# Moving the last pair sums of w_down out of the gates-and-branches stage of a fused attention and feed-forward block

## The chip, the cores and the metric

The kernel runs on one core of one Trainium2 chip. The metric is the device time of one execution in microseconds (us), the median over several runs. Each core has a TensorE (PE) for matrix products, VectorE (DVE), ScalarE (ACT), GpSimd (POOL) and SyncE (SP); all work from their own queues of instructions, in order, and wait for one another by semaphores. In this kernel SP does nothing but issue transfers between the chip's large memory (HBM) and the on-chip memory, one queue of them in program order.

## The reference

One layer of a hybrid block on 256 tokens of width 2048, all in float32:

```
h = rms_norm(x, g_mix); proj = h @ w_in            # queries, keys, values, gates
o_fox = forgetting attention, 6 heads               # softmax with a decaying bias
o_sb  = stick-breaking attention, 6 heads
o_mem = attention over 256 memory tokens, 4 heads
g = sigmoid(gates + b_gate)                          # three gates of width 2048
merged = g0 * (o_fox @ w_br_fox) + g1 * (o_sb @ w_br_sb) + g2 * (o_mem @ w_br_mem)
x = x + merged @ w_out
h2 = rms_norm(x, g_ffn)
u = causal_depthwise_conv(h2 @ w_up)                 # 3 taps, 11264 channels
x = x + (silu(u_gate) * u_val) @ w_down              # w_down is 5632 x 2048
```

## The kernel before

Every float32 product is made of three faster products: a weight tile `raw` is rounded on ACT to `hi` (L143, L379), DVE takes the rest `lo = raw - hi` (L144, L380), and PE multiplies hi by hi, hi by lo and lo by hi into one accumulator (`three`, L385 to L387; the up stage, L1365 and L1366, leaves a part out). So a weight tile goes through four queues: SP loads it into one of four `raw` buffers, ACT and DVE make `hi` and `lo` in four buffers each, PE uses them. SP may load tile n+4 only when DVE is done with tile n, and ACT may make `hi` n+4 only when PE is done with n.

The stages follow one another on PE: the memory's keys and values (`kv`), the projections `mq`, `f0` to `f4` (forgetting), `s0` to `s4` (stick-breaking; `s4`, the last, is half as wide), the first products of the branches `b`, six gate blocks `g` with the other branch products between and after them, `w_out` (`o`), the up stage (`u`, 22 groups of 4 x 128 channels, 8 pairs of weight rows each), and `w_down` (`d`).

**Pair sums.** In `o` and `d` (and in the gates) some pairs of weight row-tiles ("pairs") are multiplied with seven block products in place of eight, by the scheme of Strassen and Winograd. This wants sums of the blocks of the weights. For `o` and `d` they are made long before: a pair of 128 x 1024 weight tiles (1 MB) is loaded into a staging tile, DVE makes the four sums with three additions (`sums_in`, L254 to L256), and the tile is written back to HBM (`kept_d...`), from where the stages `o` and `d` load it (L473, L476, L478). 37 pairs are made so; the last two of `d` are summed by transfers alone (`sums_in_hbm`). The queue `halves` fixes their order: first 10 pairs of `o`, then `d` 0, 1, 2 and so on.

A **tick** is one step of the weight loop: each `product` calls `tick()` once per loaded piece, and each generator in `background` then makes one step. Three of them eat from `halves`, after one pair (`first_sums`) in the projection `mq`:

- `pair_sums_ahead(in_turn, PF, 3, 7, most=14)` in the projections `f` and `s`: a new pair every 6 or 5 ticks in turn (`PF`), loaded into one of the two halves of `staged`, its sums 3 ticks after the load, its store 7 ticks after it.
- `half_sums(..., 6, 2, 4, ...)` beside the gates and branches: half a pair at a time (two loads of 256 KB, three shorter additions, one store of 512 KB), four times, in the tile with the tag `pre`, which the stage `o` uses later as one of its `raw` buffers.
- `pair_sums_ahead(ends_tile, (15,) + (8,) * 20, 1, 5, delay=DU)` in the up stage: the first pair at tick 7, the second 15 ticks later, then one every 8 ticks; sums 1 tick and store 5 ticks after the load. There is one staging tile (`ends`, named `pre_d...`), so a load waits until the store before it has landed.

A scheduler sets each engine's order from the program's order and its own estimates; what goes through `in_order` or `pin` keeps its place among its like.

In the first steps of the up stage the kernel also computes the rows' norm of `x` (L632 to L637), writes it to HBM (`rstd_row`, L1233, 1 KB, a POOL transfer) and reads it back spread over all partitions (`rbc`, L1234). The first convolutions (L1310) need `rbc`.

Of the kernel before, what the change touches and what calls it, by code (L numbers as in the profile page):

```python
# [10 lines left out]
F32 = mybir.dt.float32  # L11
# [5 lines left out]
P = 128  # L17
# [18 lines left out]
SBUFS = 4  # L36
BLOCKS = 14
GS = 3
PF = (6, 5)
DU = 7  # L40


@with_exitstack
def hybrid_block(
# [57 lines left out]
    background = []  # L102
# [18 lines left out]
    def until(*names):  # L121
        while not issued.issuperset(names):
            yield
# [128 lines left out]
    def sums_in(w):  # L252
        both = w[:, 1:2].to_broadcast([P, 2, w.shape[2]])
        in_order(nc.vector.tensor_tensor(w[:, 0:2], w[:, 0:4:3], both, ALU.add))  # L254
        in_order(nc.vector.tensor_tensor(w[:, T2], w[:, T1], w[:, T2], ALU.add))
        in_order(nc.vector.tensor_tensor(w[:, T4], w[:, T2], w[:, T4], ALU.add))  # L256

    def kept_for(name, nb, pr):
        if (name, nb, pr) not in sums_of:
            at = f"kept_{name}{nb}_{pr}"  # L260
            sums_of[name, nb, pr] = dram.tile([P, 4, 512], F32, tag=at, name=at)
        return sums_of[name, nb, pr]

    def half_sums(staging, period, add, store, starts):

        for start in starts:
            yield from until(*start)
            name, wv, nb, pr, h = halves.popleft()
            kept = kept_for(name, nb, pr)
            w = staging(f"pre_{name}{nb}_{pr}_{h}").rearrange("p (i c) -> p i c", i=4)  # L270
            n0 = nb * PIECE + h * 256
            for n in range(2):
                in_order(
                    nc.sync.dma_start(
                        w.rearrange("p (k n) c -> p k n c", k=2)[:, :, n],
                        wv[:, 2 * pr : 2 * pr + 2, n0 + n * 512 : n0 + n * 512 + 256],
                    )
                )
            for _ in range(add):
                yield  # L280
            sums_in(w)
            for _ in range(store - add):
                yield
            in_order(nc.sync.dma_start(kept[:, :, h * 256 : (h + 1) * 256], w))
            for _ in range(period - store):
                yield

    def pair_sums_ahead(staging, period, add, store, most=99, delay=0):

        due = deque()  # L290
        clock = 0
        for _ in range(delay):
            yield

        def step():
            while due and due[0][0] <= clock:
                _, kept, w = due.popleft()
                in_order(nc.sync.dma_start(kept, w))

        periods = cycle(period if isinstance(period, tuple) else (period,))  # L300
        while len(halves) > 1 and halves[0][-1] == 0 and most:
            most -= 1
            name, wv, nb, pr, _ = halves.popleft()
            halves.popleft()
            kept = kept_for(name, nb, pr)
            w = staging(f"pre_{name}{nb}_{pr}")
            in_order(
                nc.sync.dma_start(
                    w.rearrange("p (k c) -> p k c", k=2), wv[:, 2 * pr : 2 * pr + 2, nb * PIECE : (nb + 1) * PIECE]
                )  # L310
            )
            w = w.rearrange("p (i c) -> p i c", i=4)
            due.append((clock + store, kept, w))
            for t in range(next(periods)):
                if t == add:
                    sums_in(w)
                step()
                clock += 1
                yield
        while due:  # L320
            step()
            clock += 1
            yield
# [342 lines left out]
    gp = mix.enter_context(tc.tile_pool(name="gp", bufs=3))  # L666

    def block(name, dt=F32):
        return bp.tile([P, 1024], dt, tag="blk", name=name)

    def heads_of(b):
        return b.rearrange("p (h s) -> p h s", h=4)
# [212 lines left out]
        turn[0] += 1  # L885
        return staged[:, turn[0] % 2]

    background.append(pair_sums_ahead(in_turn, PF, 3, 7, most=14))
    qm = [heads_of(block(f"qm_{i}", F32R)) for i in "hl"]
    y = norm_heads(ps, rstd, "mq")  # L890
    later(heads_T(y, qm[0], (gh[:, 2:3], gh[:, 2:3]), 2, "mq", qm[1]))
# [182 lines left out]
    def x_sums():  # L1074
        yield
        for p in range(GS):
            pair_sums(xT.pair(p), (junk(f"xa_{p}"), junk(f"xr_{p}")), [(xs[:, p], slice(0, 4))])
            for _ in range(3):
                yield

    background.append(x_sums())
    background.append(
        half_sums(lambda name: gp.tile([P, 1024], F32, tag="pre", bufs=1, name=name), 6, 2, 4, ((), (), ("second",), ()))
    )


    mT = [None] * (KT // 2)
# [164 lines left out]
    for nb, plan in enumerate(o_plans):  # L1252
# [18 lines left out]
    ends = []  # L1271
    ends_tile = lambda name, dt: ff.tile([P, 2, PIECE], dt, tag="ends", bufs=1, name=name)
    background.append(
        pair_sums_ahead(lambda name: ends_tile(name, F32).rearrange("p i c -> p (i c)"), (15,) + (8,) * 20, 1, 5, delay=DU)
    )
    a_done = []
    background.append(last_sums(148, 12))
# [72 lines left out]
    for f0 in range(0, FT, 4):  # L1350
# [5 lines left out]
        for s in range(2):  # L1356
            ps = [bank(f"u{f0 + i}_{s}") for i in range(4)]
            c0 = s * D_FF + f0 * P
            for k in range(0, KT, 2):
                hi, lo = piece(upv[:, k : k + 2, c0 : c0 + 512], 2, 512, f"u{f0}_{s}_{k}")  # L1360
                for j in range(2):
                    first, last = k + j == 0, k + j == KT - 1
                    for i in range(4):
                        c = slice(i * P, (i + 1) * P)
# [63 lines left out]
    for nb, plan in enumerate(d_plans):  # L1428
# [5 lines left out]
        for t in range(NT):  # L1434
            for n in range(2):
                c = nb * PIECE + n * 512
                o = xres[:, t, c : c + 512]
                nc.vector.tensor_tensor(o, o, X[t][n], ALU.add)
                if (nb, t, n) == (1, 1, 1):
                    nc.scalar.dma_start(ov[:, t, c : c + 256], o[:, :256])  # L1440
                    c, o = c + 256, o[:, 256:]
# [35 lines left out]
```

## Time and profile before

| what | value |
|---|---|
| runs | median 1453.27 us of 3 (1453.22 to 1453.76) |
| the profiled execution | 1453.81 us, of it 1452.1 us from the first to the last instruction (span) |
| granted TensorE clock | 1.000 |
| PE busy | 1447.0 us, 100% of the span |
| PE loading weights | 1225.8 us, 84% |
| DVE busy | 1247.5 us, 86% |
| ACT busy | 870.1 us, 60% |
| transfers | 393.41 MB, mean 271 GB/s |
| `pre_d` loads of half_sums | 8 of 256 KB, median 4.0 us from issue to landing |
| `pre_d` loads of the up stage | 18 of 1024 KB, median 7.4 us |
| `kept_d` stores of the up stage | 18 of 1024 KB, median 6.1 us |

The profile is of one execution. Its own time, 1453.81 us, is 1.7 us more than its span and 0.5 us above the median of the runs. In a row such as `L254 DVE TENSOR_TENSOR pre_d<-pre_d x22: 677/1218/1221, 313.0 to 1152.1`, the parts are the line, the engine, the operation, the tile written and the tile read, the count, the shortest, middle and longest duration in ns, and the starts of the first and the last in us. In a timeline row the first number is the start, the second the duration, both in us, and brackets hold the idle time of the engine before it with what ended it.

### The profile page before, as it was taken

What the parts mean: (1) busy time and instruction counts of PE and PEld (TensorE: products, weight loads), DVE (VectorE), ACT (ScalarE), POOL (GpSimd) and SP (SyncE); (2) the same over time, 40 slices, a digit from 0 to 9 for tenths busy, and PEclk for the clock granted to TensorE, in tenths of its full rate; (3) what the DMA queues carried; (4) which work ended last, traced back from release to release, by engine and by line L of the source; (5) the groups of instructions that cost most, each with busy time, mean ns of one, the idle gap of its engine ahead of it and who ended that gap; (6) DMA issues with size and microseconds to landing.
All of it is one profiled execution on the core that took longest, in us unless ns stands there. A gap on an engine that the chain in (4) does not pass through costs nothing.

```text
span 1452.1 us, 20709 instructions
## 1 busy us (share of the span) xinstructions
PE 1447.0 (100%) x7298; PEld 1225.8 (84%) x7298; DVE 1247.5 (86%) x1851; ACT 870.1 (60%) x1248; POOL 32.3 (2%) x70
## 2 busy tenths in 40 slices
PE   9999999999999999999999999999999999999998
PEld 7888888888888888888888888888888888888887
DVE  5888778777999999998897888888888877999988
ACT  6755445465555555546676656556556556676775
POOL 0000011010000000000000000000000011000000
PEclk9999999999999999999999999999999999999999
DMA  8797899775677676788877888888888899789996
GB/s 296 228 350 269 309 336 321 266 250 182 214 219 230 202 219 207 265 267 278 289 231 264 302 273 292 284 267 303 288 275 298 274 252 262 251 286 345 317 341 236
DMA packets 165783, 393.41 MB, mean 271 GB/s; under 512 B 12859, under 2 KB 28111, under 8 KB 161327
## 3 DMA queue, kind: packets, MB, share of 16 engines
q1 hardware_dynamic: 162190, 384.86, 79.3%
q0 software_dynamic: 2160, 5.12, 1.8%
q10 hardware_dynamic: 1328, 2.11, 0.4%
q8 instruction: 57, 0.93, 0.2%
q14 instruction: 48, 0.39, 0.1%
HBM read 353.24 MB, written 43.00 MB: 273 GB/s over the span
## 4 chain that ended last, share of the span: by engine, by line
PE 98%; DMA 1%; ACT 0%; DVE 0%; issue 0%; DVEq 0%; ACTq 0%
PE u L1365 22%; PE u L1366 11%; PE xg L387 5%; PE xg L386 5%; PE xg L385 5%; PE xd L387 3%; PE xd L386 3%; PE xd L385 3%; PE s L385 2%; PE s L387 2%; PE f L385 2%; PE f L386 2%; PE f L387 2%; PE s L386 2%; PE b L387 2%; PE b L386 2%
## 5 line engine op out<-in xcount | busy, mean ns | idle before, releaser
L1365 PE MATMUL u<-hT,hi_u 128*128 128x512 f32 x1232 | 428.4, 394 | 0.0
L1366 PE MATMUL u<-hT,lo_u 128*128 128x256 f32 x1232 | 341.3, 277 | 0.0
L1365 PEld LDWEIGHTS u<-hT,hi_u 128*128 128x128 f32 x1232 | 231.0, 188 | 53.6
L144 DVE TENSOR_TENSOR lo_u<-raw_u,hi_u 128x1024 fp32r<-128x1024 f32 x176 | 215.1, 1222 | 69.4 <-ACT hi_u L143 69.3
L143 ACT CAST hi_u<-raw_u 128x1024 fp32r<-128x1024 f32 x176 | 184.6, 1050 | 131.5 <-PE u L1365 105.1
L1366 PEld LDWEIGHTS u<-hT,lo_u 128*128 128x128 f32 x1232 | 231.3, 188 | 0.0
L379 ACT CAST hi_g<-raw_g 128x1024 fp32r<-128x1024 f32 (+1 forms) x96 | 92.5, 973 | 54.0 <-PE xg L386 23.7
L380 DVE TENSOR_TENSOR lo_d<-raw_d,hi_d 128x1024 fp32r<-128x1024 f32 x88 | 106.8, 1222 | 12.3 <-ACT hi_d L379 6.9
L379 ACT CAST hi_d<-raw_d 128x1024 fp32r<-128x1024 f32 x88 | 91.7, 1054 | 35.8 <-PE xd L386 12.2
L380 DVE TENSOR_TENSOR lo_g<-raw_g,hi_g 128x1024 fp32r<-128x1024 f32 (+1 forms) x96 | 106.4, 1119 | 4.1 <-ACT hi_g L379 3.6
L385 PE MATMUL xg<-hi_g,xT 128*128 128x512 f32 x210 | 82.0, 390 | 0.0
L387 PE MATMUL xg<-lo_g,xT 128*128 128x512 f32 x210 | 81.8, 389 | 0.0
L386 PE MATMUL xg<-hi_g,xT 128*128 128x512 f32 x210 | 81.7, 389 | 0.0
L379 ACT CAST hi_t_g<-t_g 128x1024 fp32r<-128x1024 f32 x36 | 37.9, 1053 | 48.7 <-PE xg L386 41.4
L143 ACT CAST hi_f<-raw_f 128x1024 fp32r<-128x1024 f32 (+1 forms) x40 | 38.6, 968 | 39.9 <-PE f L386 23.7
L1365 PE MATMUL u<-hT_rest,hi_u 128*128 128x512 f32 x176 | 62.0, 394 | 0.0
L144 DVE TENSOR_TENSOR lo_s<-raw_s,hi_s 128x1024 fp32r<-128x1024 f32 (+1 forms) x40 | 44.6, 1123 | 18.5 <-ACT hi_s L143 18.5
L1315 ACT ACTIVATE y<-u,taps 128x256 f32<-128x256 f32 x88 | 49.6, 596 | 17.5 <-DVE u L1310 17.4
L143 ACT CAST hi_s<-raw_s 128x1024 fp32r<-128x1024 f32 (+1 forms) x40 | 38.3, 960 | 32.5 <-PE s L386 19.5
L380 DVE TENSOR_TENSOR lo_t_g<-t_g,hi_t_g 128x1024 fp32r<-128x1024 f32 x36 | 43.6, 1221 | 14.7 <-ACT hi_t_g L379 14.6
L144 DVE TENSOR_TENSOR lo_f<-raw_f,hi_f 128x1024 fp32r<-128x1024 f32 (+1 forms) x40 | 44.4, 1117 | 13.8 <-ACT hi_f L143 13.6
L379 ACT CAST hi_t_d<-raw_t_d 128x1024 fp32r<-128x1024 f32 (+1 forms) x54 | 43.5, 835 | 19.1 <-PE xd L386 11.7
(556 smaller groups left out, 3496.3 us busy)
## 6 DMA issues: line engine op xcount, KB each, us to landing
raw_u<-in_w_up_dram SPq DMA_DIRECT2D x176, 512.0 KB, 5.0
raw_g<-in_w_in_dram SPq DMA_DIRECT2D x96, 512.0 KB, 4.4
raw_d<-in_w_down_dram SPq DMA_DIRECT2D x61, 512.0 KB, 5.6
pre_d<-in_w_down_dram SPq DMA_DIRECT2D x18, 1024.0 KB, 7.4
kept_d<-pre_d SPq DMA_DIRECT2D x18, 1024.0 KB, 6.1
raw_f<-in_w_in_dram SPq DMA_DIRECT2D x32, 512.0 KB, 5.8
raw_s<-in_w_in_dram SPq DMA_DIRECT2D x32, 512.0 KB, 6.1
raw_t_d<-kept_d SPq DMA_DIRECT2D x27, 512.0 KB, 6.7
```

Source lines behind the costliest of these rows:

```text
L143: pin(nc.scalar.copy(hi[:, :m], raw[:, :m]))
L144: pin(nc.vector.tensor_tensor(lo[:, :m], raw[:, :m], hi[:, :m].bitcast(F32), ALU.subtract))
L379: nc.scalar.copy(hi[:, :n], src)
L380: nc.vector.tensor_tensor(lo[:, :n], src, hi[:, :n].bitcast(F32), ALU.subtract)
L385: fix(nc.tensor.matmul(o, lhsT=ah, rhs=w[0], start=first, stop=False))
L386: fix(nc.tensor.matmul(o, lhsT=al, rhs=w[0], start=False, stop=False))
L387: fix(nc.tensor.matmul(o, lhsT=ah, rhs=w[1], start=False, stop=last))
L1315: nc.scalar.activation(y, u[:, 2:], AF.Identity, scale=tap(2), bias=tap(3))
L1365: nc.tensor.matmul(ps[i], lhsT=hi[:, j, c], rhs=hT(k + j), start=first, stop=False)
L1366: nc.tensor.matmul(ps[i][:, :S], lhsT=lo[:, j, c], rhs=hT(k + j)[:, :S], start=False, stop=last)
```

## The change

Three numbers and one line change. The two pairs that `half_sums` made beside the gates and branches are made elsewhere: the generator in the projections makes 15 pairs in place of 14, and the one in the up stage 19 in place of 18.

```
-PF = (6, 5)
-DU = 7
+PF = (6, 5) * 5 + (6,) + (5,) * 4
+DU = 6
...
-    background.append(pair_sums_ahead(in_turn, PF, 3, 7, most=14))
+    background.append(pair_sums_ahead(in_turn, PF, 3, 7, most=15))
...
-    background.append(
-        half_sums(lambda name: gp.tile([P, 1024], F32, tag="pre", bufs=1, name=name), 6, 2, 4, ((), (), ("second",), ()))
-    )
...
-        pair_sums_ahead(lambda name: ends_tile(name, F32).rearrange("p i c -> p (i c)"), (15,) + (8,) * 20, 1, 5, delay=DU)
+        pair_sums_ahead(lambda name: ends_tile(name, F32).rearrange("p i c -> p (i c)"), (7, 9) + (8,) * 20, 1, 5, delay=DU)
```

In ticks: the pairs of the projections start at the same ticks as before up to the thirteenth, the fourteenth (`d` 4) one tick earlier, and the new fifteenth (`d` 5) five ticks after it, in `s4`. In the up stage the pairs start at ticks 6, 13, 22, 30 and so on, before at 7, 22, 30 and so on; so `d` 6 and `d` 7 stand where `d` 7 alone stood, and from `d` 8 on nothing moves. Line numbers above 1082 are smaller by 3 in the changed kernel.

PE's instructions stand in the same order before and after. On the other engines two places differ most.

**The end of the stick-breaking projections.** SP's queue there, before (`raw_s` are tiles of `s4`, `raw_b` of the first branch products, `staged` a pair's load, `kept_d_4` its store, `pre_d_5_0` the first half-pair):

```order
L142 DMA raw_s_8_2994<-in_w_in_dram 128x2x256
L142 DMA raw_s_10_3012<-in_w_in_dram 128x2x256
L142 DMA raw_s_12_3030<-in_w_in_dram 128x2x256
L142 DMA raw_s_14_3048<-in_w_in_dram 128x2x256
L142 DMA raw_b_0_0_3073<-in_w_br_fox_dram 128x2x512
L298 DMA kept_d_4_2925<-staged 128x2048
L274 DMA pre_d_5_0_3092<-in_w_down_dram 128x2x256 x2
L142 DMA raw_b_0_2_3107<-in_w_br_fox_dram 128x2x512
```

And now:

```order
L142 DMA raw_s_8_2994<-in_w_in_dram 128x2x256
L308 DMA staged<-in_w_down_dram 128x2x1024
L142 DMA raw_s_10_3014<-in_w_in_dram 128x2x256
L142 DMA raw_s_12_3032<-in_w_in_dram 128x2x256
L298 DMA kept_d_4_2884<-staged 128x2048
L142 DMA raw_s_14_3051<-in_w_in_dram 128x2x256
L142 DMA raw_b_0_0_3079<-in_w_br_fox_dram 128x2x512
L142 DMA raw_b_0_2_3109<-in_w_br_fox_dram 128x2x512
L142 DMA raw_b_0_4_3168<-in_w_br_fox_dram 128x2x512
L142 DMA raw_b_0_0_3191<-in_w_br_fox_dram 128x2x512
L142 DMA raw_b_0_2_3209<-in_w_br_fox_dram 128x2x512
L298 DMA kept_d_5_3012<-staged 128x2048
```

The load of pair `d` 5 stands three tiles of `s4` ahead of the first branch tiles, and its store after five of them. DVE at the same place, before:

```order
L144 TENSOR_TENSOR lo_s_10_3014<-raw_s_10_3012,hi_s_10_3013 128x512
L144 TENSOR_TENSOR lo_s_12_3032<-raw_s_12_3030,hi_s_12_3031 128x512
L144 TENSOR_TENSOR lo_s_14_3050<-raw_s_14_3048,hi_s_14_3049 128x512
L144 TENSOR_TENSOR lo_b_0_0_3075<-raw_b_0_0_3073,hi_b_0_0_3074 128x1024
L403 TENSOR_TENSOR xs<-xr_3126,xs 128x4x128
```

And now:

```order
L144 TENSOR_TENSOR lo_s_10_3016<-raw_s_10_3014,hi_s_10_3015 128x512
L144 TENSOR_TENSOR lo_s_12_3034<-raw_s_12_3032,hi_s_12_3033 128x512
L144 TENSOR_TENSOR lo_s_14_3053<-raw_s_14_3051,hi_s_14_3052 128x512
L254 TENSOR_TENSOR staged<-staged 128x1024
L255 TENSOR_TENSOR staged<-staged 128x512
L144 TENSOR_TENSOR lo_b_0_0_3081<-raw_b_0_0_3079,hi_b_0_0_3080 128x1024
L256 TENSOR_TENSOR staged<-staged 128x512
L144 TENSOR_TENSOR lo_b_0_2_3111<-raw_b_0_2_3109,hi_b_0_2_3110 128x1024
```

Two of the three sums of `d` 5 stand ahead of the first branch tile's `lo`.

**The first steps of the up stage.** SP before (`raw_u_1_*` are the weights of the second half-group of the first four channel tiles; `raw_t_d` loads kept sums for `w_down` ahead of time):

```order
L142 DMA raw_u_1_6_7190<-in_w_up_dram 128x2x512
L478 DMA raw_t_d_0_12107<-kept_d_0_2285 128x512
L478 DMA raw_t_d_1_12198<-kept_d_1_2443 128x512
L142 DMA raw_u_1_8_7212<-in_w_up_dram 128x2x512
L142 DMA raw_u_1_10_7235<-in_w_up_dram 128x2x512
L298 DMA kept_d_7_7098<-pre_d_7_7099 128x2048
L142 DMA raw_u_1_12_7257<-in_w_up_dram 128x2x512
L142 DMA raw_u_1_14_7284<-in_w_up_dram 128x2x512
```

And now:

```order
L478 DMA raw_t_d_0_12090<-kept_d_0_2285 128x512
L478 DMA raw_t_d_1_12181<-kept_d_1_2443 128x512
L142 DMA raw_u_1_6_7166<-in_w_up_dram 128x2x512
L142 DMA raw_u_1_8_7189<-in_w_up_dram 128x2x512
L298 DMA kept_d_6_7052<-pre_d_6_7053 128x2048
L142 DMA raw_u_1_10_7211<-in_w_up_dram 128x2x512
L142 DMA raw_u_1_12_7236<-in_w_up_dram 128x2x512
L308 DMA pre_d_7_7234<-in_w_down_dram 128x2x1024
L142 DMA raw_u_1_14_7266<-in_w_up_dram 128x2x512
```

The load of `d` 7, which waits for the store of `d` 6 to land, now stands ahead of `raw_u_1_14`. (The first load, of `d` 7 before and of `d` 6 now, stands one tile earlier, ahead of `raw_u_0_14`.) DVE before:

```order
L144 TENSOR_TENSOR lo_u_0_14_7078<-raw_u_0_14_7076,hi_u_0_14_7077 128x1024
L635 TENSOR_TENSOR nwt_f<-nwy_f 128x2
L636 SCALAR_TENSOR_TENSOR nwt_f<-nwt_f,nwa_f 128x2
L637 SCALAR_TENSOR_TENSOR scales<-nwt_f,nwy_f 128x2
L144 TENSOR_TENSOR lo_u_1_0_7107<-raw_u_1_0_7105,hi_u_1_0_7106 128x1024
L254 TENSOR_TENSOR pre_d_7_7099<-pre_d_7_7099 128x1024
L255 TENSOR_TENSOR pre_d_7_7099<-pre_d_7_7099 128x512
L144 TENSOR_TENSOR lo_u_1_2_7142<-raw_u_1_2_7140,hi_u_1_2_7141 128x1024
L256 TENSOR_TENSOR pre_d_7_7099<-pre_d_7_7099 128x512
```

Now, first around the same tiles and then, further on, around `lo_u_1_14`:

```order
L144 TENSOR_TENSOR lo_u_0_14_7057<-raw_u_0_14_7055,hi_u_0_14_7056 128x1024
L254 TENSOR_TENSOR pre_d_6_7053<-pre_d_6_7053 128x1024
L635 TENSOR_TENSOR nwt_f<-nwy_f 128x2
L255 TENSOR_TENSOR pre_d_6_7053<-pre_d_6_7053 128x512
L636 SCALAR_TENSOR_TENSOR nwt_f<-nwt_f,nwa_f 128x2
L144 TENSOR_TENSOR lo_u_1_0_7086<-raw_u_1_0_7084,hi_u_1_0_7085 128x1024
L637 SCALAR_TENSOR_TENSOR scales<-nwt_f,nwy_f 128x2
```

```order
L144 TENSOR_TENSOR lo_u_1_12_7238<-raw_u_1_12_7236,hi_u_1_12_7237 128x1024
L254 TENSOR_TENSOR pre_d_7_7234<-pre_d_7_7234 128x1024
L255 TENSOR_TENSOR pre_d_7_7234<-pre_d_7_7234 128x512
L144 TENSOR_TENSOR lo_u_1_14_7268<-raw_u_1_14_7266,hi_u_1_14_7267 128x1024
L256 TENSOR_TENSOR pre_d_7_7234<-pre_d_7_7234 128x512
```

The norm of the rows (L637) now comes after two sums and one `lo`, and the sums of `d` 7 stand ahead of `lo_u_1_14`.

Between these places the twelve transfers and twelve additions of `half_sums` are gone. With the tile `pre` free earlier, one 512 KB load of stage `o` (`raw_t_o_3`) now stands in SP's queue right after the first tile of `s4`, before at the start of stage `o`; and the first half of the reload of `x` (`xres_again`, 1 MB) stands four tiles earlier than before, after the first branch tile of the second half.

## The prediction

> **What bounds the kernel now.** I read the page first, then who waited for whom on PE, then the chain of waits, then the stretches in which the change moves something.
>
> ```profile
> span 1452.1 us, 20709 instructions
> ...
> PE 1447.0 (100%) x7298; PEld 1225.8 (84%) x7298; DVE 1247.5 (86%) x1851; ACT 870.1 (60%) x1248; POOL 32.3 (2%) x70
> ...
> PEclk9999999999999999999999999999999999999999
> ...
> PE 98%; DMA 1%; ACT 0%; DVE 0%; issue 0%; DVEq 0%; ACTq 0%
> ```
>
> PE is busy for all but 5.1 us, its clock is whole, and 98% of the chain that ended last runs on it. The list of waits has one entry for PE in the whole run, at the start:
>
> ```profile
> PE spare L93 <- DVE qscale L590: 1.2, 1, 1.2
> ```
>
> Matmuls overlap, so a late operand could hide in one that looks long. So I look at durations, first in the branch products without sums beside them (466 to 483 us), then with half-pair sums beside them (609 to 638 us), then over the up stage, in whose last part no sums are made:
>
> ```profile
> L385 PE MATMUL b<-hi_b,oT 128*128 128x512 f32 x24 | 9.3, 389 | 0.0
> L385 PE MATMUL b<-hi_b,oT 128*128 128x512 f32 x43 | 16.7, 389 | 0.0
> L1365 PE MATMUL u<-hT_rest,hi_u x176: 392/394/395, 758.4 to 1226.7; 128*128 128x512 f32 x176
> ```
>
> 389 ns with sums and without them; in the up stage 392 to 395 ns over 176 of them. So the stream of sums takes nothing from PE's pace, neither where it is removed nor where it is added. The chain of waits leaves PE in one place in the middle of the run, in stage `o`; the timeline shows its price:
>
> ```profile
> 714.35 8.38 DMA raw_t_o<-kept_o
> ...
> 723.91 1.24 DVE lo_t_o L380
> ...
> 724.69 0.39 PE L386 MATMUL yo<-hi_t_o,ms 128*128 128x512 f32 x1
> 725.19 0.50 PE L387 MATMUL yo<-lo_t_o,ms 128*128 128x512 f32 x1
> 725.53 0.40 PE L385 MATMUL yo<-hi_t_o,ms 128*128 128x512 f32 x1
> 725.76 0.39 PE L386 MATMUL yo<-hi_t_o,ms 128*128 128x512 f32 x1
> ```
>
> Matmuls start 0.23 us apart (725.53 to 725.76). Here the steps are 0.50 and 0.34 us, so a transfer of 8.38 us cost PE 0.27 + 0.11 = 0.38 us. It was issued in `o`, where the change leaves SP's order as it was.
>
> **The change, part by part.**
>
> *Removed beside gates and branches.* The rows of the sums and of their transfers:
>
> ```profile
> L254 DVE TENSOR_TENSOR pre_d<-pre_d x22: 677/1218/1221, 313.0 to 1152.1; 128x1024 f32<-128x1024 f32 x18, 128x512 f32<-128x512 f32 x4
> L255 DVE TENSOR_TENSOR pre_d<-pre_d x22: 410/686/694, 315.4 to 1153.6; 128x512 f32<-128x512 f32 x18, 128x256 f32<-128x256 f32 x4
> L256 DVE TENSOR_TENSOR pre_d<-pre_d x22: 413/684/689, 316.9 to 1155.3; 128x512 f32<-128x512 f32 x18, 128x256 f32<-128x256 f32 x4
> ...
> pre_d<-in_w_down_dram SPq DMA_DIRECT2D x18, 1024.0 KB, 7.4
> kept_d<-pre_d SPq DMA_DIRECT2D x18, 1024.0 KB, 6.1
> ```
>
> The shortest durations are those of the half pairs: 4 x (0.68 + 0.41 + 0.41) = 6.0 us of DVE go, with 12 transfers. All of it lay beside matmuls at 389 ns that waited for nothing: 0 us. The earlier half of `xres_again` must wait for PE's last use of `xs`, and the next branch tile is queued behind it:
>
> ```profile
> L387 PE MATMUL yg<-lo_t_g,xs x1: 389/389/389, 598.1 to 598.1; 128*128 128x512 f32 x1
> ...
> 598.85 0.37 SPq L142 DMA_DIRECT2D raw_b<-in_w_br_fox_dram  x1
> ```
>
> `xs` is free at 598.5 us, and the tile went out at 598.85: 0 us as well.
>
> *Added: two whole pairs,* each 1.22 + 0.69 + 0.68 = 2.6 us of DVE, 1 MB in and 1 MB out. They cost nothing while what stands behind them reaches PE in time. So I look for the deadlines.
>
> *Pair `d` 5, at the end of the stick-breaking projections.* DVE and the first use of what is behind it:
>
> ```profile
> 302.12 0.69 DVE L144 TENSOR_TENSOR lo_s<-raw_s,hi_s 128x512 fp32r<-128x512 f32 x1 [0.75 <-ACT hi_s L143]
> 304.23 1.23 DVE L144 TENSOR_TENSOR lo_b<-raw_b,hi_b 128x1024 fp32r<-128x1024 f32 x1 [1.42 <-ACT hi_b L143]
> ...
> L387 PEld LDWEIGHTS b<-lo_b,oT x28: 187/188/188, 307.3 to 329.7; 128*128 128x128 f32 x28
> ...
> 288.26 7.32 SPq L142 DMA_DIRECT2D raw_s<-in_w_in_dram  x4
> ...
> staged<-in_w_down_dram SPq DMA_DIRECT2D x5, 1024.0 KB, 6.5
> ```
>
> DVE is idle for 1.42 us where two of the sums now go: they run from 302.8 to 304.7 us, `lo_b` then ends at 305.95, and PE wants it at 307.3: 1.35 us to spare. The load follows `raw_s_8`, issued at 288.26 us, and lands 6.5 us later, near 295, with 7 us to spare; the tiles behind it are delayed by less than that load, and they are used from 300 us on. 0 us.
>
> *Pairs `d` 6 and `d` 7, in the first steps of the up stage.* Here is the tightest place.
>
> ```profile
> 751.24 1.23 DVE L144 TENSOR_TENSOR lo_u<-raw_u,hi_u 128x1024 fp32r<-128x1024 f32 x1 [0.56 <-ACT hi_u L143]
> 754.27 0.16 DVE L635 TENSOR_TENSOR nwt_f<-nwy_f 128x2 f32<-128x2 f32 x1 [1.81 <-ACT nwy_f L634]
> ...
> 754.66 0.16 DVE L637 SCALAR_TENSOR_TENSOR scales<-nwt_f,nwy_f 128x2 f32<-128x2 f32 x1
> ...
> 777.05 1.22 DVE L144 TENSOR_TENSOR lo_u<-raw_u,hi_u 128x1024 fp32r<-128x1024 f32 x1
> ...
> 780.56 0.19 PEld L1366 LDWEIGHTS u<-hT_rest,lo_u 128*128 128x128 f32 x1
> ...
> 760.06 0.34 SPq L298 DMA_DIRECT2D kept_d<-pre_d  x1
> ...
> 756.00:764.00 8.00, 8.00 (x48) 7.00 (x48) 7.68 (x11) 4.08 (x7) 0.06 (x1) 1.00 0.63 81
> 764.00:772.00 8.00, 8.00 (x48) 7.00 (x47) 2.45 (x2) 2.10 (x2) 0.50 (x1) 1.00 0.95 333
> ...
> raw_u<-in_w_up_dram SPq DMA_DIRECT2D x4, 512.0 KB, 11.5
> ...
> raw_u<-in_w_up_dram SPq DMA_DIRECT2D x176, 512.0 KB, 5.0
> L143 ACT CAST hi_u<-raw_u x176: 1031/1051/1061, 731.0 to 1216.1; 128x1024 fp32r<-128x1024 f32 x176
> ```
>
> The last two numbers of a window row are the transfers' share and GB/s. From 756 to 764 us only 81 GB/s move: the 1 KB `rstd_row` goes out then, and tiles of 512 KB issued between 760 and 773 us take 11.5 us, where the median of all is 5.0. The first sum of `d` 6 uses the idle 1.81 us after `lo_u_0_14` (ends 752.5); the second, and one `lo`, come before L637, which thus ends at about 756.6 in place of 754.8 us. That moves `rstd_row` and the slow stretch by 1.8 us. The store of `d` 6 goes out at about 757.4 us, after its third sum.
>
> The load of `d` 7 waits on SP until that store has landed, and `raw_u_1_14` is queued behind it; on DVE its first two sums stand ahead of `lo_u_1_14`, which PE wants at 780.56 us. So DVE must begin them by 780.56 - 1.22 - 0.69 - 1.22 = 777.4 us. The store's landing is bounded from below by 6.1 us (its median), from above by 11.5 us (a transfer in the slow stretch): 763.5 to 768.9 us. The load then lands 7.4 us later, at 770.9 to 776.3 us: 6.5 or 1.1 us to spare. `raw_u_1_14`, behind it at 333 GB/s, lands 1.6 us after it, at 777.9 us at the latest; `hi` (1.05 us) and `lo` (1.22 us) end at 780.2, with 0.4 us to spare. So 0 us from either end, by a small margin at the far one. Which end is nearer, two rows on packets tell: the slow stretch (758 to 764 us), and one before it (184 to 188 us) in which a store of the same form as that of `d` 6 was in flight beside another small write:
>
> ```profile
> DMA packets 134, 0.27 MB, mean 45 GB/s; under 512 B 1, under 2 KB 1, under 8 KB 134
> ...
> DMA packets 118, 0.97 MB, mean 242 GB/s; under 512 B 0, under 2 KB 0, under 8 KB 0
> ```
>
> 22 packets per us of 2 KB there, 30 of 8 KB here: what is scarce is turns, not bytes. The store has 128 packets; at 22 per us it takes 5.8 us, so I take the near end. (The Trainium skill, DMA: Bandwidth & Descriptors, Queues, rings and completion order, says that each engine takes turns between its queues packet by packet. By that rule the store would be through in about 6 us as well, and the sum would be the same; had it been shared by bytes, 45 GB/s would make a store of some 20 us and a stall of 8 us.)
>
> *Sum.* 0 us, against the profiled execution's 1453.81 us, which lies 0.54 us above the median of the runs; so 1453.3 us is forecast for the median. About 0.2%, 2.9 us, is what can be told from no change; 1.35, 0.4 and 6.5 us are the margins, 0.38 us all there is to win.
>
> **The rivals.**
>
> *A jam in the first steps of the up stage (slower).* The store of `d` 6 is longer under way than any transfer of the trace. For it: the moved `rstd_row` may now meet a queue with a 1 MB store in front, and its own time may grow. Against it: the packets' rates. From a landing at 769.3 us on (11.9 us), PE loses what exceeds that: at 15 us 3.1 us, 1456.4 us; at 20 us 8 us. It passes 0.2% at 14.8 us.
>
> *The `lo` of the first branch tiles comes late (slower, little).* The 1.35 us of margin are used up by 3 us of delay in DVE or in tiles behind the 1 MB load: 1.7 us, 1455.0 us. Against it: ACT has those tiles' `hi` ready only as PE frees buffers.
>
> *The stall in `o` goes.* The early `raw_t_o_3` and the missing stores change how transfers meet there: 0.38 us, 1452.9 us.
>
> *PE's own pace rises without the stream (faster).* If DVE's additions and 4 MB of transfers had slowed the matmuls of the 330 us of gates and branches by 1%, their removal would give 3.3 us: 1450.0 us. Against it: 389 and 389 ns. (The Trainium skill, Trainium Kernel Development and Optimization, Best Practices, says to judge the distance to the limit by the share of weight loads, not of matmuls; by that rule 84% leaves room under PE's 100%, and a change beside PE could pay. No row shows this room being lost to the sums.)
>
> **How the numbers follow.** No measurable change 0.82; the stall in `o` gone 0.05; the jam 0.08, of which 0.05 beyond 0.2%; the branch tiles late 0.03, of which 0.01 beyond; PE's pace 0.02. So faster 0.02, same 0.92, slower 0.06. The range runs from the stall gone with a quiet run, 1452.6 us, to a late branch tile, 1455.0 us.
>
> **What would show it.** In the changed kernel's profile PE should have no wait but the first, `b` matmuls 389 ns, `hT_rest` matmuls within 392 to 395 ns; no `pre_d` sums between 310 and 640 us; L637 near 756.6 us; the load of `d` 7 issued near 764 us, and its first sum directly after `lo_u_1_12`. I am wrong if PE shows a gap near 780 us with `lo_u` behind L254, or near 307 us behind `staged`, or if matmul durations differ.

## The result, and the profile after

| | before | after |
|---|---|---|
| median of 9 runs | 1453.35 us | 1456.82 us |
| all 9 | 1452.82 to 1454.04 | six from 1456.16 to 1457.43; three from 1465.25 to 1466.33 |
| profiled execution | 1453.81 us, span 1452.1 | 1456.58 us, span 1454.9 |

The changed kernel is slower: ratio 1.0043 (95% interval 1.0023 to 1.0063). My forecast was no change, 1453.3 us with a range to 1455.0, so it was wrong. There are two costs to explain: some 3 us in every run, and some 9 us more in one run of three. The profiled execution is one of the shorter ones. Two single runs of the experiments below, 1464.06 us at a granted clock of 0.95 and 2727.91 us at 0.83, are left out of what is said of them.

Of its page, the lines that were shown of the kernel before:

```profile
span 1454.9 us, 20692 instructions
...
PE 1448.3 (100%) x7298; PEld 1229.1 (84%) x7298; DVE 1246.4 (86%) x1845; ACT 869.4 (60%) x1248; POOL 31.9 (2%) x70
...
PEclk9999999999999999999999999999999999999999
...
PE 96%; DMA 2%; DVE 1%; ACT 1%; issue 0%; SPq 0%; ACTq 0%; DVEq 0%
```

The busy shares say nothing; the chain of waits does: PE's share of it went from 98 to 96%. The list of PE's waits has a new entry (us in total, times, longest). The waits of SP and POOL that matter here, from 740 to 815 us (POOL's was 8.1 us before):

```profile
PE u L1363 <- DVE lo_u L144: 1.5, 2, 0.8
...
PE spare L93 <- DVE qscale L590: 1.2, 1, 1.2
```

```profile
SPq L308 <- DMA kept_d<-pre_d: 9.7, 1, 9.7
...
POOL rbc L1231 <- DMA rstd_row<-scales: 13.4, 1, 13.4
```

The chain of waits shows where it leaves PE (start, length, what), the timeline of PE what it costs there:

```profile
756.84 13.69 DMA kept_d<-pre_d
771.02 8.21 DMA raw_u<-in_w_up_dram
779.33 1.06 ACT hi_u L143
...
789.19 1.23 DVE lo_u L144
...
803.41 1.14 DVE pre_d L254
...
807.21 1.15 DVE lo_u L144
```

```profile
780.43 0.49 PE L1362 MATMUL u<-hT_rest,hi_u 128*128 128x512 f32 x1
781.69 0.39 PE L1363 MATMUL u<-hT_rest,lo_u 128*128 128x256 f32 x1 [0.77 <-DVE lo_u L144]
...
789.94 0.40 PE L1362 MATMUL u<-hT,hi_u 128*128 128x512 f32 x1
790.47 0.38 PE L1363 MATMUL u<-hT,lo_u 128*128 128x256 f32 x1
...
807.30 0.39 PE L1362 MATMUL u<-hT,hi_u 128*128 128x512 f32 x1
808.40 0.39 PE L1363 MATMUL u<-hT,lo_u 128*128 128x256 f32 x1 [0.71 <-DVE lo_u L144]
```

A step from the start of an L1362 matmul to the start of the next matmul is normally 0.23 us. Here three steps are 1.26, 0.53 and 1.10 us: 1.03 + 0.30 + 0.87 = 2.2 us lost, and with the slightly long steps beside them 2.7. Laid over one another matmul by matmul, the two traces differ by over 0.1 us in only two more places behind the start: at 724.7 us the changed kernel wins 0.4, and between 790 and 805 us it loses 0.3 in very small steps, on which more below. The store of `d` 6 was 13.69 us under way, and SP stood 9.7 us for it ahead of `d` 7's load and `raw_u_1_14`. The stretches of the prediction, again (last two columns: transfers' share, GB/s):

```profile
756.00:764.00 8.00, 8.00 (x49) 7.00 (x48) 5.79 (x10) 4.07 (x8) 0.74 (x1) 1.00 1.13 208
764.00:772.00 8.00, 8.00 (x49) 7.00 (x48) 1.23 (x1) 1.00 (x2) 0.55 (x1) 1.00 0.78 124
```

In the kernel before, the slow stretch was over at 764 us (333 GB/s after it). Now it begins later and reaches beyond 769 us. In both stretches together 2.7 MB move, before 3.3.

### The profile page after: what moved, and what is told of

Same layout as the page of the kernel before. It is cut to its first block, busy times and chain, and to the rows that moved or that the text cites. A ratio compares the mean times of both kernels' runs of the same rounds, so it can differ in the third digit from the quotient of the medians.

```text
span 1454.9 us, 20692 instructions
## 1 busy us (share of the span) xinstructions
PE 1448.3 (100%) x7298; PEld 1229.1 (84%) x7298; DVE 1246.4 (86%) x1845; ACT 869.4 (60%) x1248; POOL 31.9 (2%) x70
## 4 chain that ended last, share of the span: by engine, by line
PE 96%; DMA 2%; DVE 1%; ACT 1%; issue 0%; SPq 0%; ACTq 0%; DVEq 0%
PE u L1362 20%; PE u L1363 10%; PE xg L386 5%; PE xg L387 5%; PE xg L385 5%; PE xd L386 3%; PE xd L385 3%; PE xd L387 3%; PE s L387 2%; PE s L385 2%; PE f L385 2%; PE f L387 2%; PE s L386 2%; PE f L386 2%; PE b L385 2%; PE b L386 2%
## 5 line engine op out<-in xcount | busy, mean ns | idle before, releaser
L1362 PE MATMUL u<-hT,hi_u 128*128 128x512 f32 x1232 | 428.8, 392 | 0.0
L1363 PE MATMUL u<-hT,lo_u 128*128 128x256 f32 x1232 | 344.9, 280 | 0.8 <-DVE lo_u L144 0.7
L1362 PEld LDWEIGHTS u<-hT,hi_u 128*128 128x128 f32 x1232 | 230.5, 187 | 50.9
L1362 PE MATMUL u<-hT_rest,hi_u 128*128 128x512 f32 x176 | 62.2, 392 | 0.0
L144 DVE TENSOR_TENSOR lo_f<-raw_f,hi_f 128x1024 fp32r<-128x1024 f32 (+1 forms) x40 | 44.3, 1115 | 15.9 <-ACT hi_f L143 15.8
```

Of the source, the lines that this page charges most:

```text
L144: pin(nc.vector.tensor_tensor(lo[:, :m], raw[:, :m], hi[:, :m].bitcast(F32), ALU.subtract))
L1362: nc.tensor.matmul(ps[i], lhsT=hi[:, j, c], rhs=hT(k + j), start=first, stop=False)
L1363: nc.tensor.matmul(ps[i][:, :S], lhsT=lo[:, j, c], rhs=hT(k + j)[:, :S], start=False, stop=last)
```

## The experiments

Each is compared with other runs of the kernel before on the same chip.

**Which part of the change costs.** The first kernel takes the projections' part alone, the second the up stage's alone; in both, the remaining pair is made as two halves beside the gates.

```
# projections alone: the changed kernel with
+    background.append(half_sums(..., 6, 2, 4, ((), ())))
-DU = 6            ... (7, 9) + (8,) * 20
+DU = 7            ... (15,) + (8,) * 20
# up stage alone: the changed kernel with
+    background.append(half_sums(..., 6, 2, 4, ((), ())))
-PF = (6, 5) * 5 + (6,) + (5,) * 4     most=15
+PF = (6, 5)                           most=14
```

> The projections' part alone: d5 moves to the end of the projections, d6 is made as two halves beside the gates, the up stage is as in the kernel before (18 pairs). Theory A (the loss arises only in the first steps of the up stage, where the store of d6 meets the rstd_row store): no change, 1453.3 us within 0.5, the rstd_row store 8 us long, PE with no wait but the first. Theory D (the projections' pair or the earlier raw_t_o load costs part of it): 1454 us or more, with PE steps over 389 ns near 307 us or in stage o.

Measured: 1454.2 us against 1454.01, ratio 1.0005 (0.9997 to 1.0014), 11 runs, none over 1456.2. `rstd_row` is issued at 756.50 us, as late as in the changed kernel, and lands after 8.18 us: the later moment alone does not lengthen it.

> The up stage's part alone: 19 pairs there at ticks 6, 13, 22 and so on, d5 made as two halves beside the gates, the projections as before. Theory A: the whole loss, about 1456.5 us, the store of d6 some 13 us under way, SP waiting near 10 us ahead of the load of d7, PE late near 780 us; and in some runs some 9 us more, as in 3 of the 9 runs of the changed kernel. Theory D: part of the loss, 1454 to 1455.5 us.

Measured: ratio 1.0059 (1.0036 to 1.0081); six runs, 1457.27, 1459.16, 1460.78, 1466.54, 1466.7 and 1468.27 us. The store of `d` 6 was 14.65 us under way. So within the noise the whole loss, and both of its forms, come from the up stage. The runs at 1459.16 and 1460.78 us lie between the two forms; they have no profile, and what they lose is not shown. (The profiled run is one of the long ones, which the last group of experiments uses.)

**The pieces of `rstd_row`.** Its 1 KB is written as 256 pieces of 4 bytes, since the two numbers of a row lie in one partition. Here DVE turns them first:

```
+            wide, tall = (cst.tile([P, 32], F32, ...) for i in "wt")
+            nc.vector.memset(wide, 0.0)
+            nc.vector.tensor_copy(wide[:, :NT], rstd_f)
+            nc.vector.transpose(tall, wide)
-            nc.gpsimd.dma_start(row.rearrange("t p -> p t"), rstd_f)
+            for b in range(P // 32):
+                nc.gpsimd.dma_start(row[:, 32 * b : 32 * (b + 1)], tall[32 * b : 32 * b + NT])
```

> The changed kernel, with the two columns of the rows' norm turned on DVE (two small operations more, one 32 by 32 turn), so that the 1 KB of rstd_row goes out in 8 pieces of 128 bytes instead of 256 of 4 bytes. Theory A in its strong form (the slow stretch is made by the 4-byte pieces): no slow stretch, d6's store lands in 6 to 7 us, PE has no stall near 780 us, 1453.0 us (0.4 less than the kernel before where the stall in o is gone), and no run near 1465. Rival B (the stretch is made by the 1 MB store or by what else is in the queues, the small pieces only wait in it; what costs is the load of d7 ahead of raw_u_1_14): store still 13 us, 1456.5 us. Rival C (one pair more for DVE in the first steps): 1456.5 us or more, since DVE has two operations more.

Measured: 1454.03 us against 1454.01, ratio 1.0 (0.9992 to 1.0009); 11 runs, none over 1455.84. PE has no wait in the up stage, and the same two waits and stretches read:

```profile
SPq L308 <- DMA kept_d<-pre_d: 2.2, 1, 2.2
...
POOL rbc L1236 <- DMA rstd_row<-row_t: 5.7, 1, 5.7
```

```profile
756.00:764.00 8.00, 8.00 (x47) 6.96 (x46) 6.46 (x12) 4.29 (x7) 2.02 (x4) 1.00 0.83 282
764.00:772.00 8.00, 8.00 (x48) 6.98 (x47) 3.72 (x5) 3.16 (x3) 0.57 (x1) 1.00 1.00 355
```

The small pieces are a necessary part of it: 19 pairs in the up stage, the load of `d` 7 still behind the landing of `d` 6's store, but without the small pieces no loss. Rivals B and C fall. The forecast 1453.0 was 1 us low against a chip whose kernel before ran at 1454.0.

**Is it SP's wait, or the stretch?**

```
-(7, 9) + (8,) * 20
+(9, 7) + (8,) * 20
```

> The changed kernel with (9, 7) in place of (7, 9): the load of d7 stands two tiles later in SP's queue, behind raw_u_1_14. As many pairs in the first steps as in the changed kernel, d6 and rstd_row meet as there. Theory A: the slow stretch stays (store of d6 13 to 14 us), but raw_u_1_14 is no longer behind the waiting load and lo_u_1_14 not behind d7's sums: the stall near 780 us goes, 1453.5 to 1454.5 us; the runs some 9 us longer may stay. Rival C (too many sums for DVE in the first steps, wherever they stand): 1456.5 us. If the slow stretch alone, without SP's wait, starved PE: 1456 us as well, with PE waiting for raw_u tiles.

Measured: ratio 1.0056 (1.0035 to 1.0078); 1457.02, 1457.72, 1459.32, 1465.71, 1465.99, 1466.64 us. I had expected the stall to go. In the profiled run, one of the long ones:

```profile
POOL rbc L1231 <- DMA rstd_row<-scales: 15.8, 1, 15.8
```

```profile
ACT hi_u L143 <- DMA raw_u<-in_w_up_dram: 9.4, 2, 9.1
PE u L1363 <- DVE lo_u L144: 2.9, 3, 1.3
DVE u L1307 <- DMA rbc<-rstd_row: 2.3, 1, 2.3
```

Nothing stands behind a waiting load there until `raw_u_1_14` is out, and PE still waits: the stretch itself holds the `raw_u` tiles up, and ACT waits 9.1 us for one of them. SP's wait, on which my prediction spent its deadlines, is not needed for the loss. The stretch also delays `rbc`: the first convolution, at 775.02 us in the kernel before, starts here at 780.00 us, and the chain of waits leads from PE's wait at 786 us through that convolution back to `rstd_row`. So DVE is behind with convolutions as well as with `lo` tiles. No run here separates the two.

**Where the store stands.** Two kernels: the pair earlier, so that its store goes out at 753.58 us, ahead of `rstd_row`; and the store later, at 770.81 us.

```
# earlier
-DU = 6    (7, 9) + (8,) * 20
+DU = 3    (10, 9) + (8,) * 20
# store later
-(7, 9) + (8,) * 20, 1, 5, delay=DU)
+(16,) + (8,) * 20, 1, 5, delay=DU, first=6)   # the first store six ticks later
```

> The changed kernel with DU = 3 and (10, 9): d6's load is asked for at tick 3 instead of 6, its store stands two raw_u tiles earlier in SP's queue (near 752 us), so most of it is out before rstd_row's 4-byte pieces start near 756.5 us. As many pairs, the same small pieces. Theory A (the store of d6 and the small pieces hold each other up): rstd_row back to about 8 us, no late lo_u, 1453 to 1454.5 us. A rival, that the small pieces jam as long whatever is beside them: 1456 us or more.

Measured: ratio 1.0053 (1.0037 to 1.0069), five runs from 1462.25 to 1465.01 us and one of 1456.33. The forecast was wrong: the stretch stays long although the store of `d` 6 has landed by 759.86 us.

```profile
POOL rbc L1231 <- DMA rstd_row<-scales: 11.7, 1, 11.7
```

```profile
806.02 0.39 PE L1362 MATMUL u<-hT,hi_u 128*128 128x512 f32 x1
807.05 0.39 PE L1363 MATMUL u<-hT,lo_u 128*128 128x256 f32 x1 [0.63 <-DVE lo_u L144]
```

`rstd_row` is issued here at 757.56 us, so the store shares the queues with it for 2.3 us at most. At 759.86 us the next 1 MB transfer follows, the load of `d` 7. Which of the two lengthens `rstd_row` this run cannot tell.

This profile shows the second wait by itself: no stall near 780 us, yet one at 807. DVE, busy for 86% of the span, has not worked off what was left undone while tiles were late, when at 802.05 us the sums of `d` 8 come on top.

> The changed kernel with the first pair's store six ticks later (near 777 us in place of 757), and the second pair 16 ticks after the first, so that the pairs stand at ticks 6, 22, 30 and so on: still 19 pairs in the up stage and d6's load and sums where the changed kernel has them, but no 1 MB store in the queues when the 4-byte pieces go out, and one pair of sums less before 785 us. If the store beside the small pieces makes the stretch long: rstd_row 7.5 to 9 us as in the kernel before, no wait of PE in the up stage, 1453.5 to 1454.5 us, no run over 1460. If the stretch is as long without the store (12 us or more): PE waits near 780 or 805 us, 1456 us or more, some runs over 1460.

Measured: 1453.55 us against 1453.65, ratio 1.0001 (0.9992 to 1.001); 11 runs, none over 1455.57, and PE without a wait in the up stage.

```profile
POOL rbc L1232 <- DMA rstd_row<-scales: 8.2, 1, 8.2
```

With the store out of its way `rstd_row` takes 8.2 us, as before the change (8.1). So small pieces alone make a stretch of some 8 us, which the kernel bears. With the 1 MB store issued 0.3 us after them it is 13.4 to 15.8 us (the changed kernel, the up stage's part alone, the load of `d` 7 later), which it does not. This kernel also makes the second pair nine ticks later; that the second pair is not what costs is shown by the kernel with `rstd_row` in rows, which has it in the changed kernel's place.

**What in the small pieces.** First, twice as many of them, in two tiles, in the kernel before; then, in the kernel before with `rstd_row` in 8 pieces, one unread store of 256 pieces of 4 bytes, close together and 512 bytes apart.

```
+            other = dram.tile([NT, P], F32, tag="other_row", name="other_row")
+            nc.gpsimd.dma_start(other.rearrange("t p -> p t"), rstd_f)
# apart:
+            other = dram.tile([NT, P, 128], F32, tag="other_row", name="other_row")
+            nc.gpsimd.dma_start(other[:, :, 0].rearrange("t p -> p t"), rstd_f)
```

> The kernel before, with a second 1 KB store of the same 4-byte form ahead of rstd_row's, into a tile that nobody reads. Theory A (the small pieces make the slow stretch): the stretch of 8 us grows to some 16, raw_u tiles come late, PE loses 3 to 8 us, or 10 to 16 where PE also falls into the slower rhythm (399 in place of 394 ns for an L1365 matmul). Rival B (small pieces only suffer; the large store makes the stretch): no change, 1453.3 to 1454 us.

Measured: 12 runs, seven from 1452.99 to 1455.95 us, five from 1463.19 to 1466.09; ratio 1.0031 (1.001 to 1.0052). The profiled run is a short one. In it the stretch did not double, so neither forecast came whole:

```profile
756.00:764.00 8.00, 8.00 (x49) 7.00 (x48) 7.06 (x10) 3.45 (x7) 0.00 (x0) 1.00 0.85 82
764.00:772.00 8.00, 8.00 (x49) 7.00 (x48) 2.45 (x2) 2.11 (x2) 0.57 (x1) 1.00 0.89 326
```

82 and 326 GB/s, before 81 and 333. So the length of the stretch does not follow the number of pieces. The five long runs have no profile; that the kernel before stands near the edge is my reading of them, and not shown.

> The kernel before with rstd_row in 8 pieces of 128 bytes, and ahead of it a store of the 1 KB in 256 pieces of 4 bytes into a tile that nobody reads, one piece beside the other. Nothing waits for it, so only what it does to other transfers is seen. If pieces of 4 bytes make the stretch: some 8 us at 50 to 110 GB/s from 755 us on, raw_u tiles 11 us under way, 1453.5 to 1454.5 us. If it is what waits for rstd_row (the read, the first convolutions) that makes the stretch: none, over 200 GB/s throughout.

> As the run with the unread store of 256 pieces of 4 bytes, but each piece in a stretch of 512 bytes of its own, so that no two pieces fall close to one another in HBM. If it is their number or their size that holds up the other transfers: the same stretch of some 8 us at 50 to 110 GB/s. If it is that they all fall into the same 1 KB: no stretch, over 200 GB/s throughout.

Measured: 1454.11 us (ratio 1.0003, 0.9995 to 1.0012) with the pieces close together, 1453.66 us (median of nine runs, the kernel before 1453.65) with them apart. The stretches, first close, then apart:

```profile
756.00:760.00 4.00, 4.00 (x25) 3.48 (x24) 3.97 (x5) 1.49 (x3) 1.39 (x3) 1.00 0.74 85
760.00:764.00 4.00, 4.00 (x25) 3.48 (x24) 3.23 (x6) 2.10 (x5) 0.00 (x0) 1.00 0.61 37
```

```profile
756.00:760.00 4.00, 4.00 (x25) 3.52 (x24) 3.97 (x6) 1.57 (x2) 1.65 (x4) 1.00 0.64 211
760.00:764.00 4.00, 4.00 (x25) 3.48 (x24) 3.50 (x6) 2.50 (x6) 0.57 (x1) 1.00 0.85 292
```

The same 256 pieces of 4 bytes, from the same place, issued at 754.63 and 754.90 us: 85 and 37 GB/s when they fall into one 1 KB, 211 and 292 GB/s when each has 512 bytes of its own. So neither their number nor their size alone holds up the other transfers; that many small writes go to the same small piece of HBM does. Why this stops others, and why a large store makes it longer, these runs do not show.

**The runs some 9 us longer.** The up stage from 850 to 1220 us, the L1362/L1365 matmuls of the kernel before, of the changed one (short run), and of the up stage's part alone (long run); count, busy us, mean ns:

```profile
L1365 PE MATMUL u<-hT,hi_u 128*128 128x512 f32 x940 | 326.6, 394 | 0.0
...
L1365 PE MATMUL u<-hT_rest,hi_u 128*128 128x512 f32 x128 | 45.1, 394 | 0.0
```

```profile
L1362 PE MATMUL u<-hT,hi_u 128*128 128x512 f32 x932 | 323.8, 391 | 0.0
...
L1362 PE MATMUL u<-hT_rest,hi_u 128*128 128x512 f32 x136 | 47.9, 391 | 0.0
```

```profile
L1365 PE MATMUL u<-hT,hi_u 128*128 128x512 f32 x912 | 323.1, 399 | 0.0
...
L1365 PE MATMUL u<-hT_rest,hi_u 128*128 128x512 f32 x136 | 48.8, 399 | 0.0
```

In 370 us PE starts 1068, 1068 and 1048 of them: 346.4, 346.4 and 353.1 ns for a pair of matmuls, at full granted clock and with no wait. The changed kernel's short run has a piece of the slower rhythm too, from its wait at 790 us to that at 807:

```profile
L1362 PE MATMUL u<-hT,hi_u 128*128 128x512 f32 x39 | 13.8, 399 | 0.0
```

399 ns there, 391 after. That is the 0.3 us lost in small steps: the wait at 790 us brought the slower rhythm, the one at 807 took it away. In the long run it stays, from the last wait at 810 us to the stage's end at 1239: some 1200 pairs x 6.7 ns = 8.0 us, which is what the traces differ by there. In the kernel with the pair earlier a delay brought it that no list of waits has. One weight load starts 0.17 us after the one before it, where 0.11 to 0.12 is normal, since its `lo_u` was ready only at 789.06 us:

```profile
788.95 0.19 PEld L1362 LDWEIGHTS u<-hT,hi_u 128*128 128x128 f32 x1
789.12 0.19 PEld L1363 LDWEIGHTS u<-hT,lo_u 128*128 128x128 f32 x1
```

From 791 to 807 us its matmuls show the slower rhythm too, and there the wait at 807 us did not take it away:

```profile
L1362 PE MATMUL u<-hT,hi_u 128*128 128x512 f32 x36 | 12.8, 399 | 0.0
```

So PE has several rhythms for one and the same stream, and a late operand can move it from one to another. Is a wait alone enough? In the kernel before with `rstd_row` in 8 pieces one `lo_u` is computed several times:

```
-            nc.vector.tensor_tensor(lo, raw, hi, subtract)
+            for _ in range(1 + more):        # more = 4 or 2 for one tile, else 0
+                nc.vector.tensor_tensor(lo, raw, hi, subtract)
```

> The kernel before with rstd_row in 8 pieces of 128 bytes (so no slow stretch), and one lo_u of the up stage (fourth group of channel tiles, second half, fifth tile, near 900 us) computed five times in place of once: PE waits for it once or twice, some 1 to 4 us, without any jam of transfers. Theory R (the runs some 9 us longer are those in which PE, after a wait, goes on in a slower rhythm, 353 ns per pair of matmuls in place of 346, until the up stage ends): in some runs 1455 to 1457 us, in others 7 ns x 16 pairs per 5.55 us from 900 to 1224 us, 6.6 us more; a profile in that state shows 399 ns at L1366's neighbour line of hi_u matmuls from about 900 us on and 394 before. Rival J (the long runs come from transfers that jam longer): all runs within 1 us of one another, 1454 to 1457 us.

> The same as the run with the late lo near 900 us, but in the tenth group of channel tiles, near 1133 us. Theory R: the wait itself costs as much as there; the slower rhythm, where it comes, lasts only 90 us and costs 1.8 us in place of 6.6, so no run is over 1460 us. Rival J: the same times as with the wait near 900 us.

> As the run with the late lo near 900 us, with three computations of that lo in place of five: 2.4 us less of DVE, so a wait of PE of 3.9 - 2.4 = 1.5 us. Theory R (a wait may leave PE in the slower rhythm): one part of the runs 1.5 to 2 us over the kernel before, 1455.5 to 1456.5 us, the other 6 to 6.6 us above those, with nothing between but chip noise. If only waits of several us do it: all runs at 1455.5 to 1457 us.

| the late `lo` | runs, us |
|---|---|
| five times, at 905 us | 1460.01, 1460.43, 1460.46, 1462.01; 1465.43, 1466.77 |
| five times, at 1172 us | 1459.46, 1459.56, 1460.85, 1462.45, 1462.99 |
| three times, at 905 us | seven from 1453.6 to 1455.34; 1458.87, 1459.86, 1460.22, 1460.55 |

Near 905 us the runs fall into two groups, 5 to 6 us apart, without any stretch of slow transfers; near the end of the stage, where the slower rhythm has some 50 us left (1.0 us), nothing is over 1463. With six and five runs that alone would be thin, but the profile of the wait near the end shows it directly. Its `hi_u` matmuls last 393 or 394 ns up to the wait, and from 1182 us on

```profile
L1371 PE MATMUL u<-hT,hi_u 128*128 128x512 f32 x121 | 42.9, 399 | 0.0
```

with no slow stretch near it (312 to 357 GB/s from 1174 to 1180 us). A wait alone is enough, and Rival J falls. Three of my numbers were off. The wait meant for 1133 us came at 1172. The long wait cost 6.7 us instead of 1 to 4 (and 5.8 us near the end, so three of those five runs are over the forecast 1460), for a reason that the granted clock (third column from the right) shows:

```profile
PE u L1372 <- DVE lo_u L145: 3.9, 1, 3.9
```

```profile
905.00:908.00 3.00, 1.31 (x7) 0.75 (x5) 3.00 (x4) 1.05 (x1) 0.00 (x0) 1.00 0.76 182
...
912.00:914.00 2.00, 2.00 (x8) 1.71 (x7) 0.70 (x2) 0.14 (x1) 0.00 (x0) 0.50 0.98 370
```

And the shorter one nearly vanished, for a reason that I did not follow up: the profiled run, a short one, has a wait of 0.3 us of a weight load, none of a matmul. Yet from there on its matmuls last 391 ns where they had lasted 394, at the same pace, and in four of eleven runs some 5 to 6 us are lost. Those four have no profile; that they went on in the slower rhythm is argued from the sizes alone.

## Why the prediction was wrong, step by step

*Removed sums: right.* Nothing is won beside gates and branches. The `b` matmuls of the changed kernel, in the two stretches of the prediction:

```profile
L385 PE MATMUL b<-hi_b,oT 128*128 128x512 f32 x24 | 9.3, 389 | 0.0
L385 PE MATMUL b<-hi_b,oT 128*128 128x512 f32 x43 | 16.7, 389 | 0.0
```

*Pair `d` 5 at the end of the projections: right.* The forecast was two sums from 302.8 us, and `lo_b` ready at 305.95:

```profile
302.85 1.22 DVE L254 TENSOR_TENSOR staged<-staged 128x1024 f32<-128x1024 f32 x1
304.11 0.69 DVE L255 TENSOR_TENSOR staged<-staged 128x512 f32<-128x512 f32 x1
304.71 1.22 DVE L144 TENSOR_TENSOR lo_b<-raw_b,hi_b 128x1024 fp32r<-128x1024 f32 x1
```

*The stall in `o`: right in size, but not the change's doing.* It is gone here, and is worth the forecast 0.4 us. But it is gone, too, in all six profiles of kernels that are built on the kernel before. One of them, that with twice the small pieces, has up to there the same instructions in the same order on every engine. And it is present with the up stage's part alone and with the pair made earlier. So the change does not decide it; I took one execution for the kernel.

*Pairs `d` 6 and `d` 7: the step that failed.* Up to the store everything came as told (L637 forecast at 756.6; `rstd_row` issued at 756.51, the store at 756.84). Then "the store's landing is bounded from below by 6.1 us (its median), from above by 11.5 us": it took 13.69, and the near end, at "22 packets per us", was the wrong one. From 756.84 to 770.50 us 717 packets move, 52 per us, and the store's 128 still take all of that time. Both bounds came from the kernel before, in which the store of `d` 7 joins only at 760.06 us, 4.95 us after `rstd_row`:

```profile
755.11 0.74 POOL L1233 DMA_DIRECT2D rstd_row<-scales  x1 [418.96 <-DVE scales L637]
```

In the changed kernel the store of `d` 6 joins 0.33 us after it. I took the length of the slow stretch as given and moved it by 1.8 us, when the change put into its beginning the very thing that lengthens it. (The Trainium skill, DMA: Bandwidth & Descriptors, Queues, rings and completion order, has each engine take turns packet by packet; my estimate by it was some 6 us. The trace, with 13.69 us, does not agree with that estimate.) The note that "its own time may grow" stood under the rival, with 0.08.

*The rival's price was right as far as it went.* "From a landing at 769.3 us on" PE was to lose what exceeds that. The store landed at 770.53 us, 1.2 us past it, and PE lost 1.3 near 780 us. What it left out came later: the waits at 790 and 807 us, another 1.4 us. A tile's first deadline was met or missed in my sum, and then forgotten; but DVE has only 14% of its time to catch up, and the next pair's sums came before it had.

*The slower rhythm was in no step.* I had shown PE's matmuls at 392 to 395 ns as a pace that nothing moved, and rightly; that a short wait may move it for the rest of a stage, no row of the kernel before could show. It is shown in the profiles of the up stage's part alone, of the kernels with the second pair later or the first pair earlier and of the late `lo` near the stage's end, and in 17 us of the changed kernel's own; its three long runs themselves have no profile.

## What to carry to other kernels

Look for stores that put many small pieces into one small place, and count what shares the queues with them before adding a large transfer there: turned into rows, or with the large store 14 us after them, the same work costs nothing. A deadline is not one instant: after a late tile, follow the engine that catches up until its slack is back, with all that is queued for it meanwhile. And where matmuls run back to back, a delay too short for the list of waits can cost several microseconds, so compare the number of matmuls per stretch, not the waits alone.

## What the hardware showed that I had not expected

- 256 writes of 4 bytes into one 1 KB of HBM hold all other transfers of the core at 37 to 85 GB/s for some 8 us; with 512 bytes for each, the others run at 211 to 292 GB/s. Two such stores into two places at once land after 9.1 us each, one alone after 8.5.
- PE repeats the same two matmuls at 346.4 or at 353.1 ns a pair, with durations of 394, 391 or 399 ns for the longer; a late operand, down to a weight load 0.05 us late, may move it from one to another, where it stays until a later wait or the stage's end. In the 75 runs of the kernel before beside the experiments the slower one cannot be seen (all within 1452.85 to 1455.54 us). (The Trainium skill, TensorE: Matmul & The Clock Gate, Back-to-back issue gap, has the spacing set by weight load and matmul together in a window that reorders; it gives no second rhythm, and no run here shows what fixes it.)
- After a wait of 3.9 us PE went on at a granted clock of 0.50: for 5.6 us from 910 us on, which cost 2.6 us more, and for 3.4 us near 1180 us, which cost 1.6. After waits of up to 1.3 us the clock stayed at 1.00.
